# Nine small tiles requested earlier: where the large SBUF slots begin

## The chip, the core and the metric

The kernel runs on one core of a Trainium2 chip. The metric is the device time of one execution in microseconds, the median of several runs.

## What is computed

One hybrid decoder block over 256 positions of width 2048, all in fp32: a normed input and one wide projection, an S5 state-space branch and an attention branch over picked keys, both merged by gates, an output projection, a gated per-layer embedding and a last norm.

```
h = rms_norm(x, g_mix);  proj = h @ w_in            # 2048 -> 8272 columns
u, z_ssm, c_q, k, v, z_attn, k_idx, w_idx, gate_ssm, gate_attn = split(proj)
y_ssm  = s5_branch(u, ...) * silu(z_ssm)            # scan, gelu, y @ w_glu
o_ssm  = y_ssm @ w_ssm_out
cq     = rms_norm(c_q, g_q); q = cq @ w_uq; q_idx = cq @ w_uq_idx
y_attn = dsa_branch(q, k, v, q_idx, k_idx, w_idx) * silu(z_attn)
o_attn = y_attn @ w_attn_out
x = x + (sigmoid(gate_ssm) * o_ssm + sigmoid(gate_attn) * o_attn) @ w_o
e = rms_norm(p @ w_ple, g_ple_post)
x = x + sigmoid(rms_norm(x, g_ple) @ w_ple_gate) * e
return rms_norm(x, g_final)
```

## The kernel before

Every large product is made of fp32r matmuls in three parts: weights and activations are each split into a high and a low half, and high by high, high by low and low by high are accumulated in PSUM. The weights come as units of 128 x 1024 (512 KB, 4096 bytes in each partition). A unit is loaded by SyncE's queue into one of five `raw` buffers (L93 to L98), ScalarE rounds it into one of four `hi` buffers (L260), VectorE takes the rest into one of four `lo` buffers (L272), and TensorE uses both. All matmuls are recorded by one helper, `mm` (L140), all transposes by another (L148).

The main loop (L1175 to L1189) goes through the units one by one: the unit's matmuls, the `hi` of three units ahead, the deferred evictions, the `lo` of two units ahead, one more load, and then a share of the side threads (`pump`): the tables and the scan of the S5 branch (`s5_tables`, `s5_gen`, L805 and L893), the attention (`attn_gen`, L974). So each engine's order is fixed when the program is made.

A matmul here has a moving operand, which streams its columns, and a stationary one, loaded just before (LDWEIGHTS). Activations lie in the pool `cp`, in large slots that several tiles use in turn: XH and XL (the input's halves, later those of the residual sum), S1, S2, S5 of 16, 16 and 8 KB, and S4, S3, S7, kb, S6 of 8, 16, 16, 4 and 8 KB. There are two kinds of units:

- 256 columns: a block of output channels, the activations moving, 128 columns of weights stationary. XH and XL move in `block_k16` (28 blocks of 48 matmuls, before 388 us). In `block_small` (L343) S6 moves for the queries (`cq`, 16 blocks of 12 matmuls), and S7 for the GLU (`yg`, 16 blocks of 24).
- 512 columns: `block_tm` (L313), 128 positions of activations stationary, 512 columns of weights moving. XH and XL are stationary for the gates and for the last product; S3 for the SSM output (`ys`, 192 matmuls), S7 for the attention output (`ya`, 192), S5 for the embedding (`ph`, 48), and S2 with S3 for the output projection (`mh` in S2 and `ml` in S3, 384).

The first four of the last eight units keep their `hi` in S2 and their `lo` in S3 (`unit_tile`, L242).

A pool of one buffer per tag hands out bytes in the order in which tags are first requested, rounded up to 32, and a later request of the same tag gets the same bytes. A request issues no instruction. `const` (L66) and `slot` (L63) are such requests. The nine small tiles of the change are those of the last norms: `re_v`, `re_c`, `r2_v`, `r2_c` (L634 to L638), `r3v0`, `r3v1` (L690), `sqe` (L1086), `sq2` (L623), `sq3` (L657). Before, they are requested behind S6, `rcq_v`, `rcq_c` and `rowcq`.

Of the kernel before, what the change touches and what calls it, by code (L numbers as in the profile page):

```python
# [18 lines left out]
P = 128  # L19
# [10 lines left out]
NC = 4  # L30
# [13 lines left out]
def block_kernel(ctx: ExitStack, tc: tile.TileContext, A: dict, out: bass.AP):  # L44
# [14 lines left out]
    def nm(s):  # L59
        uid[0] += 1  # L60
        return f"{s}_{uid[0]}"

    def slot(tag, shape, dt=F32):  # L63
        return cp.tile(shape, dt, tag=tag, name=nm(tag))

    def const(s, shape, dt=F32):  # L66
        return cp.tile(shape, dt, tag=s, name=s)
# [142 lines left out]
    def spawn_first(gen):  # L210
        t = spawn(gen)
        threads.insert(0, threads.pop())
        return t
# [567 lines left out]
    def s5_powers():  # L781
        abr, abi = R["abar"][:, 0], R["abar"][:, 1]

        def cmul(i, xr, xi, yr, yi):
            t0, t1 = st_("er"), st_("eq")
            tt = TT
            tt(t0, xi, yi, ALU.mult)
            tt(t1, xr, yr, ALU.mult)
            tt(pre[:, i], t1, t0, ALU.subtract)
            tt(t0, xr, yi, ALU.mult)  # L790
            tt(t1, xi, yr, ALU.mult)
            tt(psi[:, i, 1], t1, t0, ALU.add)
            V.tensor_scalar(psi[:, i, 0], psi[:, i, 1], -1.0, None, ALU.mult)

        cmul(0, abr, abi, abr, abi)
        yield 1.2
        for i, a, b in ((1, 0, 0), (2, 1, 0), (3, 1, 1), (4, 3, 3), (5, 4, 3), (6, 4, 4)):
            cmul(i, pre[:, a], psi[:, a, 1], pre[:, b], psi[:, b, 1])
            yield 1.2

    def bc(ap, n):
        return ap.unsqueeze(-1).to_broadcast(list(ap.shape) + [n])


    def s5_tables():  # L805
        yield from s5_small()
        ab, f = R["abar"], R["f"]
        bp = slot("S4", [P, 2, 32, 32])
        nc.sync.dma_start(bp, A["sb"])
        ct = slot("S3", [P, 2, 2, 32, 32])  # L810
        nc.sync.dma_start(ct[:, 0, 0], A["sc"][:, 0])
        ci = slot("S7", [P, 2, 32, 32])
        nc.sync.dma_start(ci[:, 0], A["sc"][:, 1])
        yield 0.0
        bb = slot("S1", [P, 2, 32, 2, 32])

        def cmul_v(o, xr, xi, yr, yi, op):
            TT(o, xr, bc(yr, 32), ALU.mult)
            yield 1.14
            TT(ci[:, 1], xi, bc(yi, 32), ALU.mult)  # L820
            yield 1.14
            TT(o, o, ci[:, 1], op)
            yield 1.14

        br, bi = bp[:, 0], bp[:, 1]
        Br, Bi = bb[:, 0, :, 1, :], bb[:, 1, :, 1, :]
        abr, abi, nabi = ab[:, 0], ab[:, 1], ab[:, 2]
        yield from cmul_v(Br, br, bi, f[:, 0], f[:, 1], ALU.subtract)
        yield from cmul_v(Bi, bi, br, f[:, 0], f[:, 1], ALU.add)
        yield from cmul_v(bb[:, 0, :, 0, :], Br, Bi, abr, abi, ALU.subtract)  # L830
        yield from cmul_v(bb[:, 1, :, 0, :], Bi, Br, abr, abi, ALU.add)
        S.activation(ct[:, 1, 0], ci[:, 0], AF.Copy, scale=-1.0)
        R["ct"] = ct
        R["s5b"] = spawn_first(s5_states(bb))
        yield from cmul_v(ct[:, 0, 1], ct[:, 0, 0], ci[:, 0], abr, abi, ALU.subtract)
        yield from cmul_v(ct[:, 1, 1], ct[:, 0, 0], ct[:, 1, 0], nabi, abr, ALU.add)
        yield from s5_powers()
# [318 lines left out]

    R["xnorm"] = spawn(xnorm_gen(), 2)
    R["s5t"] = spawn(s5_tables(), 7)
    first_loads()
    S.activation(first, mhalf, AF.Copy)  # L1160
# [147 lines left out]
```

## Time and profile before

| | before |
|---|---|
| median of three runs | 798.55 us (798.19 to 799.98) |
| the profiled execution | 799.28 us |
| its span, first to last instruction | 797.3 us |
| TensorE (PE) busy | 776.6 us, 97% |
| VectorE (DVE) busy | 576.2 us, 72% |
| ScalarE (ACT) busy | 397.6 us, 50% |
| mean granted TensorE clock | 0.994 |

The span is what the profile sees; the 2.0 us beside it lie before and after. Busy time of PE overlaps itself, since one matmul starts before the one ahead has ended. How fast a stream of matmuls runs is read from the distance between their starts. [...]

### The profile page before, as it was taken

The page shows a single profiled execution, that of the slowest core. Times are in us where ns is not written, and L with a number is a line of the kernel's source. Part 1 is how long each engine was busy: PE and PEld are TensorE (multiplying, and loading weights), DVE is VectorE, ACT ScalarE, POOL GpSimd, SP SyncE. Part 2 cuts the span into 40 slices and gives each one's busy share as a digit, 9 for nine tenths or more (in the row PEclk, how much of TensorE's full clock was granted, in tenths as well). Part 3 has the DMA queues.
Part 4 walks back from the last instruction along what each step waited for, and adds up shares of the span by engine and source line. Part 5 has one row for each costly group of instructions (what it writes and reads, how often), then busy time and mean ns, then how long its engine had stood idle before and what let it go on. Part 6 is the DMA issues. An engine that isn't in the chain of part 4 may idle for free.

```text
span 797.3 us, 12926 instructions
## 1 busy us (share of the span) xinstructions
PE 776.6 (97%) x5080; PEld 674.5 (85%) x5080; DVE 576.2 (72%) x899; ACT 397.6 (50%) x544; POOL 8.8 (1%) x18
## 2 busy tenths in 40 slices
PE   8999999999997999999999999999999999999995
PEld 6999987777997888899999988887887888888885
DVE  6999964999999954455668887666678555456753
ACT  7544546543444744453455474544345454455642
POOL 0000000000000000000000000000000000000000
PEclk9999999999999999999999999999999999999998
DMA  8768775346662686634754556775866665556622
GB/s 318 284 211 228 232 222 179 116 162 208 213 209 92 204 259 212 220 112 146 244 179 153 189 167 221 232 247 193 266 218 219 228 204 185 176 181 195 217 86 106
DMA packets 52637, 158.08 MB, mean 198 GB/s; under 512 B 5984, under 2 KB 12128, under 8 KB 52192
## 3 DMA queue, kind: packets, MB, share of 16 engines
q1 hardware_dynamic: 47392, 150.15, 57.8%
q10 hardware_dynamic: 5184, 7.10, 2.5%
q8 instruction: 40, 0.66, 0.3%
q14 instruction: 21, 0.17, 0.1%
HBM read 147.79 MB, written 8.39 MB: 196 GB/s over the span
## 4 chain that ended last, share of the span: by engine, by line
PE 47%; issue 1%; DVE 1%; ACT 1%; DMA 1%; POOLq 0%; POOL 0%; DVEq 0%; ACTq 0%
PE main L140 44%; PE aux L140 2%; PE aux L148 1%; DMA zld<-za_d 1%; ACT S L697 0%; DVE lo L272 0%; DVE S L1087 0%; ACT hi L260 0%; ACT S L591 0%; DVE t L1045 0%; ACT S L650 0%; DVE S L649 0%; DVE S L648 0%; ACT S L645 0%; DVE S L651 0%
## 5 line engine op out<-in xcount | busy, mean ns | idle before, releaser
L272 DVE TENSOR_TENSOR lo<-raw,hi 128x1024 fp32r<-128x1024 f32 (+2 forms) x255 | 304.8, 1197 | 156.3 <-ACT hi L260 156.1
L260 ACT CAST hi<-raw 128x1024 fp32r<-128x1024 f32 (+2 forms) x255 | 261.4, 1031 | 302.9 <-PE main L140 268.3
L140 PE MATMUL main<-hi,S 128*128 128x512 f32 x544 | 175.6, 398 | 0.9 <-ACT S L1088 0.9
L140 PE MATMUL main<-lo,XH 128*128 128x512 f32 (+2 forms) x408 | 155.9, 382 | 2.4 <-DVE lo L272 2.4
L140 PE MATMUL main<-hi,XH 128*128 128x512 f32 (+2 forms) x408 | 156.9, 385 | 0.0
L140 PE MATMUL main<-hi,XL 128*128 128x512 f32 (+2 forms) x408 | 156.0, 382 | 0.0
L140 PE MATMUL main<-XH,hi 128*128 128x256 f32 x448 | 126.3, 282 | 2.7 <-ACT hi L260 2.7
L140 PE MATMUL main<-XH,lo 128*128 128x256 f32 x448 | 125.5, 280 | 1.9 <-DVE lo L272 1.9
L140 PE MATMUL main<-XL,hi 128*128 128x256 f32 x448 | 125.3, 280 | 0.0
L140 PEld LDWEIGHTS main<-hi,S 128*128 128x128 f32 x544 | 102.4, 188 | 24.8 <-ACT S L1088 1.6
L140 PE MATMUL main<-lo,S 128*128 128x512 f32 x272 | 107.5, 395 | 0.0
L140 PEld LDWEIGHTS main<-lo,XH 128*128 128x128 f32 x408 | 76.7, 188 | 19.0 <-DVE lo L272 4.6
L140 PEld LDWEIGHTS main<-hi,XH 128*128 128x128 f32 x408 | 76.6, 188 | 15.6
L140 PEld LDWEIGHTS main<-hi,XL 128*128 128x128 f32 x408 | 76.6, 188 | 14.3
L140 PEld LDWEIGHTS main<-XH,hi 128*128 128x128 f32 x448 | 84.9, 189 | 3.1 <-ACT hi L260 2.9
L140 PEld LDWEIGHTS main<-XH,lo 128*128 128x128 f32 x448 | 85.6, 191 | 2.1 <-DVE lo L272 2.1
L140 PEld LDWEIGHTS main<-XL,hi 128*128 128x128 f32 x448 | 85.0, 190 | 0.1
L140 PE MATMUL main<-S,hi 128*128 128x256 f32 x384 | 69.9, 285 | 0.1
L140 PEld LDWEIGHTS main<-lo,S 128*128 128x128 f32 x272 | 51.2, 188 | 11.1
L140 PEld LDWEIGHTS main<-S,hi 128*128 128x128 f32 x384 | 59.2, 189 | 1.7 <-issue 0.7
L140 PE MATMUL main<-S,lo 128*128 128x256 f32 x192 | 54.1, 282 | 0.0
L140 PEld LDWEIGHTS main<-S,lo 128*128 128x128 f32 x192 | 36.2, 189 | 0.0
(215 smaller groups left out, 656.4 us busy)
## 6 DMA issues: line engine op xcount, KB each, us to landing
raw<-in_wts_dram SPq DMA_DIRECT2D x247, 512.0 KB, 4.2
raw<-in_wvk_dram SPq DMA_DIRECT2D x8, 336.0 KB, 2.9
gs_d<-big ACTq DMA_DIRECT2D x8, 256.0 KB, 3.3
ga_d<-big ACTq DMA_DIRECT2D x8, 256.0 KB, 5.0
big<-gs_d SPq DMA_DIRECT2D x8, 256.0 KB, 4.4
big<-ga_d SPq DMA_DIRECT2D x8, 256.0 KB, 3.7
S<-in_grow_dram SPq DMA_DIRECT2D x2, 1024.0 KB, 7.5
big<-in_xtok_dram SPq DMA_DIRECT2D x8, 256.0 KB, 3.5
```

The source lines that it names most:

```text
L140: PE.matmul(o, l, r, start=start, stop=stop, **kw)
L148: PE.matmul(o, i, idn, is_transpose=True)
L260: S.copy(hi[:, o], src[:, o])
L272: TT(lo[:, o], src[:, o], his[u][:, o].bitcast(F32), ALU.subtract)
```

## The change

```diff
@@ def s5_tables() @@
         yield from s5_small()
         ab, f = R["abar"], R["f"]
+        for t in ("re_v", "re_c", "r2_v", "r2_c", "r3v0", "r3v1"):
+            const(t, [P, 2])
+        for t in ("sqe", "sq2"):
+            const(t, [P, 2, NC])
+        const("sq3", [P, 2, NC + 1])
         bp = slot("S4", [P, 2, 32, 32])
         nc.sync.dma_start(bp, A["sb"])
         ct = slot("S3", [P, 2, 2, 32, 32])
```

The nine tiles are requested once more, ahead of the first request of S4. They take 320 bytes there, and S4, S3, S7, kb, S6 and the three small tiles behind them move up by 320 bytes. What comes after the nine tiles' old place stays where it was. The first bytes within a partition, as the two programs have them:

```
slot                before   mod 512     after   mod 512
XH / XL      35104 / 51488       288      same       288
S1                   17728       320      same       320
S2 / S5      67872 / 84256       288      same       288
psi                  94496       288      same       288
S4                   98784       480     99104       288
S3                  106976       480    107296       288
S7                  123360       480    123680       288
kb                  139744       480    140064       288
S6                  143840       480    144160       288
rowcq               152096        32    152416       352
raw, hi, lo    from 153440       352      same       352
```

All tiles of `raw`, `hi` and `lo` are 4096 bytes apart. In both programs every engine has the same instructions in the same order, with the same waits.

## Rows read from the trace of the kernel before

**Rows 1.** The page: busy time of two engines, and the chain by line.
```profile
PE 776.6 (97%) x5080; PEld 674.5 (85%) x5080; DVE 576.2 (72%) x899; ACT 397.6 (50%) x544; POOL 8.8 (1%) x18
...
PE 47%; issue 1%; DVE 1%; ACT 1%; DMA 1%; POOLq 0%; POOL 0%; DVEq 0%; ACTq 0%
```

**Rows 2.** PE's waits from 388 to 700 us: us in total, times, longest.
```profile
PE main L140 <- ACT S L1088: 0.9, 1, 0.9
PE aux L148 <- DVE t L1045: 0.2, 1, 0.2
```

**Rows 3.** Line 140 in six windows: count, durations, first and last start, forms.
```profile
L140 PE MATMUL main<-XH,hi x139: 276/276/276, 35.8 to 82.7; 128*128 128x256 f32 x139
...
L140 PE MATMUL main<-XH,lo x74: 281/281/281, 207.9 to 233.7; 128*128 128x256 f32 x74
...
L140 PE MATMUL main<-XH,lo x57: 281/281/281, 346.9 to 366.7; 128*128 128x256 f32 x57
...
L140 PE MATMUL main<-S,lo x34: 282/285/287, 389.9 to 401.7; 128*128 128x256 f32 x34
...
L140 PE MATMUL main<-S,lo x52: 279/281/285, 430.8 to 449.0; 128*128 128x256 f32 x52
...
L140 PE MATMUL main<-lo,S x42: 392/400/400, 607.1 to 636.0; 128*128 128x512 f32 x42
```

**Rows 4.** Pieces of the chain that ended last: start, length, what, instructions.
```profile
506.76 14.00 PE main L140 x60
...
542.51 4.54 DMA zld<-za_d
...
566.94 11.19 PE main L140 x48
...
579.00 11.14 PE main L140 x48
...
638.88 22.18 PE main L140 x96
...
661.93 22.47 PE main L140 x96
...
685.27 22.11 PE main L140 x96
...
708.26 68.70 PE main L140 x300
```

**Rows 5.** Timeline of PE around 593.5 us: start, length, what.
```profile
591.78 0.40 PE L140 MATMUL main<-lo,S 128*128 128x512 f32 x1
...
593.18 0.40 PE L140 MATMUL main<-lo,S 128*128 128x512 f32 x1
...
593.88 0.39 PE L140 MATMUL main<-lo,S 128*128 128x512 f32 x1
...
595.94 0.39 PE L140 MATMUL main<-lo,S 128*128 128x512 f32 x1
```

**Rows 6.** Windows: us; busy of PE, PEld, DVE, ACT, POOL; clock, DMA, GB/s.
```profile
253.00:258.00 5.00, 0.50 (x2) 0.30 (x2) 4.96 (x8) 4.78 (x7) 0.00 (x0) 1.00 0.00 0
258.00:262.00 4.00, 3.97 (x20) 3.97 (x21) 4.00 (x6) 3.39 (x6) 0.00 (x0) 0.57 0.51 164
...
438.00:448.00 10.00, 10.00 (x86) 10.00 (x86) 9.90 (x26) 4.79 (x7) 0.66 (x1) 1.00 0.61 206
...
468.00:478.00 10.00, 10.00 (x48) 7.54 (x46) 9.79 (x21) 6.40 (x9) 0.00 (x0) 1.00 0.65 205
```

**Rows 7.** DVE: the scan's first half, its second half, slots in 206 to 262.
```profile
L915 DVE TENSOR_TENSOR S<-S,pre 128x1024 f32<-128x1024 f32 x3 | 3.7, 1223 | 0.1
...
L915 DVE TENSOR_TENSOR S<-S,pre 128x1024 f32<-128x1024 f32 x3 | 3.7, 1217 | 0.0
...
206.00:262.00 56.00, 37.42 (x72) 0.97 0.54 172
```

## The prediction

> **What bounds the kernel now.** I read the page first, then TensorE's waits, then the chain of work that ended last, and only then single stretches. On the page PE is busy 97% of the span, VectorE 72%, and the chain is a list of PE pieces with hardly anything between them [rows 1]. The waits say the same of the part of the program that uses the moved slots: from 388 to 700 us PE's matmuls waited 1.1 us in total for other engines [rows 2]. So from 388 us on the pace of back-to-back matmuls is the pace of the kernel, and a nanosecond saved per matmul is saved for good, unless another engine is found right behind.
>
> The pace is the distance from one matmul's start to the next, not its duration (276 to 400 ns, overlapped). In a row of line 140 for a window it is last start minus first start, divided by the count less one, and by three, since one operand pair in three has that name. In a piece of the chain it is length by count. Two forms matter, and each runs both on slots that move and on slots that stay:
>
> - 256 columns, the slot as the moving operand, the weight pieces hi and lo as the stationary one. On XH and XL (byte 288 modulo 512) 138 x 3 intervals from 35.8 to 82.7 us give 113.3 ns, the same form on the same bytes from 207.9 to 233.7 us gives 117.8, and from 346.9 to 366.7 us 117.9 [rows 3]. On S6 and S7 (byte 480) it is 119.2 (389.9 to 401.7 us, 33 x 3) and 119.0 (430.8 to 449.0 us, 51 x 3) [rows 3].
> - 512 columns, the slot as the stationary operand, hi and lo moving. On XH and XL 300 matmuls in 68.70 us: 229.0 ns. On S3 60 in 14.00 us: 233.3. On S7 48 in 11.19 and 48 in 11.14 us: 233.1 and 232.1. In the output projection, whose high halves lie in S2 (byte 288) and low halves in S3 (480), 96 in 22.18 and 96 in 22.47 us: 231.0 and 234.1 [rows 4].
>
> What makes these differ? Width, type, line and clock are alike. The row that tells most is a place where only the stationary slot changes in the middle of a stream: by the program's order the stationary operand is S7 (480) up to 593.5 us and S5 (288) from there, and the weights stay where they are. The starts run 591.78 to 593.18, six intervals of 233 ns, and then 593.88 to 595.94, nine of 229 [rows 5]. S5 is another slot than XH, 48 KB further on, and still has XH's pace. The pool also rotates hi and lo through four buffers 4096 bytes apart with no trace of it in the pace. So I take the byte modulo 512 as what counts.
>
> **The change, part by part.** The nine requests issue no instruction, and the order and the waits on all five engines are those of before. Nothing is added to pay for; what changes is the start byte of S4, S3, S7, kb and S6 (480 to 288 modulo 512), and of rcq_v, rcq_c and rowcq. Weights, XH, XL, S1, S2, S5 and the evictions' buffers stay.
>
> *256 columns.* The query units run on S6, 16 blocks of 12, 192 matmuls; the GLU units on S7, 16 of 24, 384. After the change their operands start on the bytes of XH and the weights. XH has two paces there, and I can't say beforehand which one a stretch will fall into: a stretch keeps the pace it enters with, and entries follow each interruption by small matmuls. Bounds: all at 117.8 gives 192 x 1.4 + 384 x 1.2 = 0.7 us, all at 113.3 gives 192 x 5.9 + 384 x 5.7 = 3.3 us. Before 388 us, of the 1344 matmuls of this form, about 560 run at the slow pace (66 us of starts: 22 to 34, 206 to 235 and 347 to 372 us, of which [rows 3] shows the cores of the latter two) and 780 at the fast one, a mean of 115.2. I take that mean: 192 x 4.0 + 384 x 3.8 = 2.2 us.
>
> *512 columns.* All XH stretches have 229.0, with no second pace. The SSM output (S3) has 192 matmuls, 192 x 4.3 = 0.8 us. The attention output (S7) 192 x 3.6 = 0.7 us. The output projection has 384: its first stretch runs at 235 (607.1 to 636.0 us, 41 x 3, read to a tenth of a us; I take 234) [rows 3], then 231.0 and 234.1 [rows 4], and the last piece, 96 in 22.11 us [rows 4] with some 38 of XH at its end, leaves 231. Weighted 232.8, so 384 x 3.8 = 1.5 us. Together 3.0 us. The 48 matmuls on S5 have the pace already.
>
> *The last eight units.* Half of their weights are kept in S2 and S3 as moving operands; S3 goes from 480 to 288, the byte of XH itself. That pair of equal bytes exists there already (S2 with XH). At most 48 matmuls of 256 columns by the 5 ns that the paces of this width differ: 0.2 us either way, taken as nothing.
>
> *Other engines.* VectorE reads two operands from slots in the scan. In the first half of it E and W both start at 480, in the second E is S1 (320) and W 480: 1223 and 1217 ns for the same 1024 elements [rows 7]. So its pace hardly knows the bytes; taken as nothing, with 0.5% of the scan's 37.4 us of slot work between 206 and 262 us [rows 7], 0.2 us, either way. [...]
>
> *What is late next.* Where PE gets faster, lo must keep up. VectorE is busy 9.90 of 10 us from 438 to 448 and 9.79 of 10 from 468 to 478 [rows 6]. The code keeps two units of lead, so a full 10 us that would have to shrink by 0.4 us is carried by the lead; if it isn't, the 256-column gain from there on is lost, at most the GLU's 1.4 us. Further down the chain holds one transfer, 4.54 us for a zld tile [rows 4]; it hangs on work that PE itself releases and so moves with it, at no cost or gain.
>
> Sum: 2.2 + 3.0 = 5.2 us. The profiled execution took 799.28 us (span 797.3 and 2.0 around it); it would become 794.1. It lies 0.7 us above the median of the three runs, 798.55, and from that the forecast is 793.3 us, 0.65% less. A measurement of this kernel can tell about 0.2% (1.6 us) from no change.
>
> **The rivals.** *Bytes don't matter to TensorE.* Its two streams would then be free of each other and the paces above would come from something else, say from what the other engines do in those stretches. Time: 798.5. For it: the same XH bytes show 113.3 and 117.8, so something beside bytes is at work. Against it: [rows 5], where the pace switches with the slot and nothing else, and a 229.0 that holds across 68.70 us of differing company [rows 4]. [...] Chance 9%; another 1% for a cancelling drift of the fast stretches before 388 us (780 matmuls at +4.5 ns would give back 3.5 us).
>
> *Only the 512-column half pays.* The query and GLU stages fall into the slow pace of XH, or VectorE's full stretches eat what they save: 3.0 us and a bit, 795.3. For it: 9.90 of 10 us in [rows 6], and the direct entry from another width at 206 us went into the slow pace. Against it: the lead of two units, and the entry at 34 us, after small matmuls as there are between the GLU units, which went into the fast one [rows 3]. Chance 20%.
>
> *Slower: VectorE pays for equal bytes.* E in S7, W in S4 and the power tables in psi would all start at 288, and in the second half W at 288 against S1 at 320. In the full stretch from 206 to 262 us any loss goes straight into PE's wait at 253 [rows 6]. Of its 37.4 us of slot work, 18% (6.8 us) is the point from which the kernel gets slower by over 0.2%; at 25%, 9.4 us less the 5.2, it would take 802.7. Against it: E and W had equal bytes before, at 0.5% [rows 7]. Chance 4%, with what else may turn up.
>
> **How the numbers follow.** Main case 66%, the half case 20%: faster 0.86. Same 0.10, slower 0.04. Range: the low end takes the fast pace throughout, 6.3 us, and about one us of slow stretches before 388 us that may turn fast, 791.0; the high end is the half case with two us of the fast stretches turned slow, 797.2.
>
> **What would show it.** In the profile after, the pieces on S3, S7 and of the output projection should read 229 ns by length over count, as XH's; if they stay at 232 to 234, bytes modulo 512 were not the cause. The query and GLU stages should read 113.3 or 117.8 and nothing between but mixtures. VectorE's two scan halves should keep 1217 to 1223 ns, and PE's gap at 253 us its size. The forecast is wrong if PE's waits for lo grow between 430 and 490 us, or if stretches before 388 us change their pace by more than the moved ones gain.

## The result and the profile after

| | before | after |
|---|---|---|
| median of five runs | 799.18 us (798.19 to 800.71) | 793.74 us (793.06 to 794.93) |
| the profiled execution | 799.28 us | 793.06 us |
| its span | 797.3 us | 791.0 us |
| mean granted TensorE clock, a share of the full one | 0.994 | 0.993 |

The ratio of after to before is 0.9936, with a 95% interval of 0.9925 to 0.9947: 5.4 us less, where 5.2 had been worked out. The forecast was 793.3 us, 0.65% less; it came to 0.64% less.

The page of after, to be held against [rows 1]: busy time by engine, and the chain by engine.

```profile
PE 770.6 (97%) x5080; PEld 671.8 (85%) x5080; DVE 576.0 (73%) x899; ACT 397.6 (50%) x544; POOL 8.8 (1%) x18
...
PE 48%; issue 1%; ACT 1%; DVE 1%; POOLq 0%; POOL 0%; ACTq 0%
```

The chain as it is printed begins at 388 us, so 48% of the span is nearly all of it. The counts are the same on every engine, and so is, to 0.2 us, the time of VectorE and ScalarE. Only PE became shorter, by 6.0 us, and its weight loads by 2.7. PE's waits from 388 to 700 us are down to one row, the first of [rows 2]:

```profile
PE main L140 <- ACT S L1093: 0.9, 1, 0.9
```

So what the matmuls saved was not handed to a wait. The chain of after, in pieces (start, length, what, instructions), answers to [rows 4]; the first piece holds the last 72 matmuls of the queries and the first 48 of the GLU, the second 168 of the GLU:

```profile
400.77 13.62 PE main L140 x120
...
427.63 19.26 PE main L140 x168
...
503.04 13.76 PE main L140 x60
...
562.26 11.00 PE main L140 x48
574.13 11.00 PE main L140 x48
...
633.23 21.99 PE main L140 x96
...
656.09 21.99 PE main L140 x96
...
678.95 21.98 PE main L140 x96
...
701.80 68.67 PE main L140 x300
```

The same two pieces before:

```profile
402.61 14.24 PE main L140 x120
...
430.22 20.13 PE main L140 x168
```

Length by count: S6 and S7 as moving operand 13.62 / 120 = 113.5 ns a matmul (before 118.7), S7 alone 19.26 / 168 = 114.6 (before 119.8; both with a first interval of 0.22 us behind small matmuls, and from 430.40 us on every interval of after is 113 or 114 ns), S3 13.76 / 60 = 229.3 (before 233.3), S7 as stationary operand 11.00 / 48 = 229.2 (before 233.1 and 232.1), the output projection 21.99 / 96 = 229.1 (before 231.0 and 234.1). XH at the end keeps 228.9. All 512-column stretches now have one pace.

The timeline of PE at the place of [rows 5], where the stationary operand changes from S7 to S5 near 588.5 us (start, length, what):

```profile
586.77 0.39 PE L140 MATMUL main<-lo,S 128*128 128x512 f32 x1
...
588.14 0.39 PE L140 MATMUL main<-lo,S 128*128 128x512 f32 x1
...
590.89 0.39 PE L140 MATMUL main<-lo,S 128*128 128x512 f32 x1
```

Six intervals from the first to the second row, on S7, give 228.3 ns, twelve more to the third, nearly all on S5, 229.2. Before, the pace switched here from 233 to 229. Now nothing is left to switch.

Where the 6.3 us of the two spans lie follows from the starts of the same chain pieces in both profiles:

| stretch | before, us | after, us | saved |
|---|---|---|---|
| up to the queries | 389.17 | 388.02 | 1.15 |
| queries and GLU | 77.40 | 75.02 | 2.38 |
| last gates, SSM and attention outputs, most of S5's units | 131.36 | 129.84 | 1.52 |
| from there to the output projection's second stretch | 7.44 + 33.51 | 7.43 + 32.92 | 0.60 |
| the rest of the output projection | 68.51 | 67.70 | 0.81 |
| last product and end | 89.91 | 90.07 | -0.16 |

The first row is not the change's. 0.5 us of it is a gap of PE at 91 us, 1.41 us from one matmul on XH to the next for 0.91 after, 0.3 of it a wait for ScalarE; `all_moved` below has that wait of 0.3 us too, with all the distances of after. The rest lies in XH's 256-column stretches, whose bytes did not move; the experiment `after_again` below shows that they differ between executions of one program. Without it the spans differ by 5.15 us.

### The profile page after: what moved, and what is told of

Read it like the earlier page. It is cut to its first block, busy times and chain, and to the rows that moved or that the text cites. A ratio compares the mean times of both kernels' runs of the same rounds, so it can differ in the third digit from the quotient of the medians.

```text
span 791.0 us, 12926 instructions
## 1 busy us (share of the span) xinstructions
PE 770.6 (97%) x5080; PEld 671.8 (85%) x5080; DVE 576.0 (73%) x899; ACT 397.6 (50%) x544; POOL 8.8 (1%) x18
## 4 chain that ended last, share of the span: by engine, by line
PE 48%; issue 1%; ACT 1%; DVE 1%; POOLq 0%; POOL 0%; ACTq 0%
PE main L140 44%; PE aux L140 2%; PE aux L148 1%; ACT S L697 0%; DVE lo L272 0%; DVE S L1092 0%; ACT hi L260 0%; ACT S L591 0%; ACT S L650 0%; DVE S L648 0%; DVE S L649 0%; ACT S L645 0%; DVE S L651 0%; POOLq L1308 0%; ACT S L1093 0%
## 5 line engine op out<-in xcount | busy, mean ns | idle before, releaser
L140 PE MATMUL main<-S,hi 128*128 128x256 f32 x384 | 67.5, 280 | 0.1
```

The costliest lines, as they stand in the source:

```text
L140: PE.matmul(o, l, r, start=start, stop=stop, **kw)
```

## Experiments

The expectations number the theories. Theory 1: the pace of a matmul on TensorE follows the distance in bytes between the start of the activations' slot and the start of the weights' buffer. Theory 2: it follows the slot's own start byte. Theory 3: bytes don't matter to TensorE. Below, *d* is the weights' start minus the slot's start, modulo 512. In the kernel before d is 64 for XH, XL, S2, S5 and 384 for S3, S6, S7; after, it is 64 for all.

**Weights moved instead of slots.** From before; a last request in the slots' pool puts 192 bytes ahead of the weights' pool, which lies behind it, so raw, hi and lo start at 32 modulo 512 (the evictions' buffers, further on, move along). Slots stay where they were: d becomes 64 for S3, S6, S7 and 256 for XH, XL, S2, S5.

```diff
     finish_half(1)
+    const("padw", [P, 48])
```

> The kernel before with all weight buffers 192 bytes further on, at byte 32 modulo 512; every slot stays (XH, XL, S2, S5 at 288, S3, S6, S7 at 480). So the weights stand 64 above S3, S6 and S7, and 256 above XH, XL, S2, S5. Theory 1 (the distance from slot to weights sets the pace): the queries and the GLU run at 113.3 or 117.8 ns, S3's and S7's 512-column matmuls at 229, as in the changed kernel, although their slots have not moved; XH's stretches get a new pace, which I can't say. Theory 2 (the slot's own byte sets it): all as before, 119 and 233 on S3, S6, S7, 113 to 118 and 229 on XH; 799 us. Theory 3 (bytes don't matter to TensorE): as before, 799 us.

Measured: 797.91 us, ratio to before 0.9987 (0.9977 to 0.9996). Pieces of its chain, in the order queries, GLU, S3, S7, output projection (twice), XH:

```profile
406.18 13.62 PE main L140 x120
...
433.04 19.25 PE main L140 x168
...
508.26 13.75 PE main L140 x60
...
568.01 11.00 PE main L140 x48
...
639.20 22.20 PE main L140 x96
...
662.27 22.20 PE main L140 x96
...
708.30 68.17 PE main L140 x300
```

The slots on byte 480 have the paces of after, to 0.01 us a piece, though not one of them moved. XH, which didn't move either, changed both its paces: 68.17 / 300 = 227.2 ns at 512 columns, less than ever before, and at 256 columns this row (line 140 in 36 to 83 us: count, durations, first and last start)

```profile
L140 PE MATMUL main<-XH,hi x131: 283/283/366, 35.9 to 82.7; 128*128 128x256 f32 x131
```

gives 46.8 us by 130 x 3 = 120.0 ns, where XH had 113.3. What S3, S6, S7 and the wide matmuls on XH gained, XH's 1344 narrow ones gave back, which is why the total hardly moved. So the slot's byte alone is not the cause, nor anything that stays fixed when only the weights move. One thing came out unexplained: in the output projection, which alternates between S2 (d = 256) and S3 (d = 64), 22.20 / 96 = 231.3 ns is slower than either distance has alone (227.2 and 229).

**Both moved.** From after; 192 bytes ahead of XH, so every slot that these matmuls read starts at 480 and the weights at 32. All distances are those of after, none of these start bytes is.

```diff
+    const("padx", [P, 48])
     xgh = slot("XH", [P, KT, T], F32R)
     xgl = slot("XL", [P, KT, T], F32R)
```

> The changed kernel with XH, XL and all behind them, weights included, 192 bytes further on: slots at 480, weights at 32 modulo 512, still 64 above. Theory 1 (distance): the paces and the time of the changed kernel, 793.7 us within 1.6. Theory 2 (the slot's own byte, 480 being the bad one): all stretches of 256 columns at 119 ns and of 512 at 233, 1920 x 4.6 ns and 1872 x 3.7 ns over the changed kernel, some 809 us. Theory 3: 794 to 799 us.

Measured: 794.63 us, ratio 0.9947 (0.9928 to 0.9965), overlapping after's interval. The pieces of the chain are after's to 0.02 us (13.62 for the queries, 13.76 for S3, 11.00 for S7, 21.99 in the output projection, 68.69 for XH). All slots at the byte that looked slow before run at the good pace. Theory 2 has fallen; theory 1 stands both ways.

**The nine tiles behind S3.** From before; the requests stand behind the one for S3, so S7, kb and S6 move and S4 and S3 don't. A part of the change alone.

```diff
         ct = slot("S3", [P, 2, 2, 32, 32])
+        for t in ("re_v", "re_c", "r2_v", "r2_c", "r3v0", "r3v1"):
+            const(t, [P, 2])
+        for t in ("sqe", "sq2"):
+            const(t, [P, 2, NC])
+        const("sq3", [P, 2, NC + 1])
```

> The nine tiles requested behind S3 instead of ahead of S4: S7, kb and S6 move to 288 as in the change, S4 and S3 stay at 480. Theories 1 and 2: the queries and the GLU gain 2.4 us and the attention output 0.7 as in the changed kernel; the SSM output (S3) stays at 233 ns and the output projection (S2 with S3) at 231 to 234, so 2.2 us of the change's gain are missing: 795 to 796.5 us. Theory 3: no such split by slot; the time lies where the company of other engines puts it.

Measured: 796.29 us, ratio 0.9969 (0.9954 to 0.9984). Chain pieces: queries, GLU, S3, S7, output projection (three times):

```profile
400.80 13.62 PE main L140 x120
427.66 19.26 PE main L140 x168
...
503.27 14.00 PE main L140 x60
...
563.63 11.00 PE main L140 x48
...
635.23 22.18 PE main L140 x96
...
658.28 22.47 PE main L140 x96
...
681.62 22.11 PE main L140 x96
```

S6 and S7 have after's lengths; S3 and the output projection have before's, to the hundredth (14.00, 22.18, 22.47, 22.11 in [rows 4]). The gain is the sum of separate gains, one for each slot and form. The median is 2.6 us below before's; the sum has 2.2 + 0.7 for S6 and S7.

**Scans of the distance.** From after; hi and lo get four fixed buffer pairs with pads between them, so that successive units of 24 (or 12) matmuls on XH run at four distances in turn, in one program. The evictions' `t` gets eight buffers for nine, to make room.

```diff
-        return wp.tile([P, 1024], F32R, tag=tag, name=nm(tag))
+        return wp.tile([P, 1024], F32R, tag=f"{tag}{u % 4}", name=nm(tag), bufs=1)
...
+    for i, n in enumerate((0, 16, 16, 16)):
+        if n:
+            wp.tile([P, n], F32, tag=f"pad{i}", name=f"pad{i}", bufs=1)
+        for t in ("hi", "lo"):
+            wp.tile([P, 1024], F32R, tag=f"{t}{i}", name=f"{t}pre{i}", bufs=1)
```

The first pad is 0, 64, 8 and 72 elements of 4 bytes in the four kernels: distances 64, 128, 192, 256; 320, 384, 448, 0; 96, 160, 224, 288; 352, 416, 480, 32.

> The changed kernel with its four pairs of weight buffers at four distances above the slots: 64, 128, 192 and 256 bytes modulo 512, by unit number modulo 4 (raw buffers behind them; eight instead of nine buffers for the evictions' products). Theory 1: within each stretch on XH the pace goes through four values in turn, and the units at 64 have 113 to 118 ns (256 columns) and 229 (512). Theories 2 and 3: one pace for all four. The time itself is not the question; somewhere from 785 to 810 us.

> As scan_64_256, with the four pairs of weight buffers 320, 384, 448 and 0 bytes above the slots (modulo 512). Theory 1 (the distance from slot to weights sets the pace): 384 gives what S3, S6 and S7 had before, 119 ns (256 columns) and 232.5 (512); 0 gives what the last eight units have where two equal bytes meet, 120 and 227; 320 and 448 are unknown, and if the pace depended on the distance without its sign they would be those of 192 (118, 233) and 64 (113 to 118, 229). Theory 2 (the slot's own byte): one pace, 113 to 118 and 229.

> As scan_64_256, with distances 96, 160, 224 and 288 (odd multiples of 32, so that a slot and the weights differ in their place within 64 bytes). If only the distance in steps of 64 counts, each behaves as a neighbour: 113 to 120 ns and 227 to 233. If the place within 64 bytes counts, a pace outside of those ranges shows.

> As scan_96_288, with distances 352, 416, 480 and 32. The same two possibilities: within 113 to 120 ns and 227 to 233, or outside.

Measured, one execution of each: 801.65, 801.83, 806.29 and 806.26 us, beside 798.6 to 798.9 for before. The paces stand in the timelines. The last matmul of five successive 256-column units, in the kernel with 64 to 256 (start, length, what):

```profile
45.93 0.28 PE L140 MATMUL main<-XH,lo 128*128 128x256 f32 x1
...
48.66 0.28 PE L140 MATMUL main<-XH,lo 128*128 128x256 f32 x1
...
51.50 0.28 PE L140 MATMUL main<-XH,lo 128*128 128x256 f32 x1
...
54.33 0.28 PE L140 MATMUL main<-XH,lo 128*128 128x256 f32 x1
...
57.21 0.28 PE L140 MATMUL main<-XH,lo 128*128 128x256 f32 x1
```

From each row to the next is the length of a unit: 2.73, 2.84, 2.83 and 2.88 us, for d = 64, 128, 192 and 256. The same five rows where d is 320, 384, 448 and 0:

```profile
45.87 0.28 PE L140 MATMUL main<-XH,lo 128*128 128x256 f32 x1
...
48.60 0.28 PE L140 MATMUL main<-XH,lo 128*128 128x256 f32 x1
...
51.44 0.28 PE L140 MATMUL main<-XH,lo 128*128 128x256 f32 x1
...
54.27 0.28 PE L140 MATMUL main<-XH,lo 128*128 128x256 f32 x1
...
57.15 0.28 PE L140 MATMUL main<-XH,lo 128*128 128x256 f32 x1
```

2.73, 2.84, 2.83 and 2.88 again, though each unit is 256 bytes further off. All sixteen distances, as the length of a unit by its matmuls, in ns:

| d modulo 256 | 0 | 32 | 64 | 96 | 128 | 160 | 192 | 224 |
|---|---|---|---|---|---|---|---|---|
| 256 columns (24) | 120.2 | 118.5 | 113.7 | 118.8 | 118.2 | 119.6 | 117.9 | 116.7 |
| 512 columns (12) | 228.3 | 233.3 | 230.3 | 234.2 | 232.9 | 233.3 | 232.9 | 233.6 |

These units lie in 36 to 83 us (256 columns) and 293 to 320 us (512). In every column two distances 256 bytes apart were run, and there their units agree to 0.01 us. So the period is 256 bytes, not 512. The sign counts: 64 and 192 differ. The best distance is another one for each form: 64 for 256 columns, 0 for 512. (A unit's length includes its passage to a neighbour with another distance; streams that stay at 0 or at 64 have 227.2 and 229.0 at 512 columns.)

**After once more.** The changed kernel itself, beside a new set of runs of before.

> The changed kernel once more, beside the two below: 793.7 us, 0.9936 of before.

Measured: 794.23 us, ratio 0.9945 (0.9932 to 0.9957). The stretch of XH from 347 us, in the profile of after and then in this one (line 140: count, durations, first and last start):

```profile
L140 PE MATMUL main<-XH,hi x57: 276/276/276, 346.7 to 365.8; 128*128 128x256 f32 x57
```

```profile
L140 PE MATMUL main<-XH,lo x55: 281/281/281, 346.8 to 365.9; 128*128 128x256 f32 x55
```

One program, the same bytes: 19.1 / (56 x 3) = 113.7 ns in one execution, 19.1 / (54 x 3) = 117.9 in the other. At 206 us before and after differ in the same way, on bytes that the change leaves alone: [rows 3] have 281 ns and 117.8 there, after has 276 and 113.0 up to 222 us. Such choices make up the other 0.6 us ahead of the queries. By the starts of the same matmuls in both profiles, after gained 0.6 us between 206 and 235 us and 0.8 between 347 and 372, and lost 0.5 between 235 and 268 us and 0.3 between 332 and 347, for the most part in stretches where it had 117.8 ns and before 113.3.

**Wide weights at distance 0.** From after; a hi or lo buffer is 256 bytes longer, and a unit of 512 columns uses it from element 48 (192 bytes) on, so that wide units have d = 0 modulo 256 and narrow ones keep 64. `t` has seven buffers.

```diff
-        return wp.tile([P, 1024], F32R, tag=tag, name=nm(tag))
+        o = 0 if units[u][3] in narrow else 48
+        return wp.tile([P, 1088], F32R, tag=tag, name=nm(tag))[:, o:o + 1024]
```

> The changed kernel, with weight buffers 256 bytes longer, in which units of 512 columns start 192 bytes later: there the weights stand 256 above the slots, in units of 256 columns 64 as before (seven instead of nine buffers for the evictions' products). By the scans (the distance counts, modulo 256; 0 is best for 512 columns at 227.2 ns, 64 for 256 columns): 1872 matmuls x 1.8 ns less than the changed kernel, 790.4 us, unless the two buffers less add a wait. If the scans' mixtures misled, 229 stays and 793.7 us.

Measured: 790.65 us (790.33 to 791.15), ratio to before 0.9899 (0.9884 to 0.9914), 3.6 us below the 794.23 of the changed kernel on the same chip. Chain pieces: S3, S7, output projection, XH:

```profile
502.09 13.62 PE main L140 x60
...
561.93 10.93 PE main L140 x48
...
632.52 21.81 PE main L140 x96
...
700.58 68.06 PE main L140 x300
```

226.9 to 227.7 ns in all of them, the queries and GLU as in after (13.61 and 19.26 us). This beats both kernels.

**Slots at distance 0.** From before; the nine tiles move ahead to other places, and instead of the weights the slots are placed: S2, S3, S5, and by an offset of 64 bytes the late tiles in S7, XH and XL, start where the weights do modulo 256. Only wide units (and the last eight) use them so; a few other requests change places to give these bytes. The weights come to lie 256 bytes further on, which is the same place modulo 256.

```diff
+    def behind(tag, off):
+        return slot(tag, [P, KT * T + 16], F32R)[:, off:off + KT * T]
...
-        ya = slot("S7", [P, 2, 8, T], F32R)
+        ya = behind("S7", 16).rearrange("p (a h t) -> p a h t", a=2, t=T)
```

> The weights where they are, and the tiles that only serve 512 columns moved to their distance 0 modulo 256 (S2, S3, S5, and inside their slots the attention output, and the residual's halves in XH and XL); those of 256 columns stay 64 below. Only the gates' 720 matmuls of 512 columns keep 229 ns: some 1150 x 1.8 ns less than the changed kernel, 791.7 us; the last eight units' 256-column matmuls stay at 120 ns.

Measured: 791.22 us (790.89 to 793.19), ratio 0.9912 (0.9899 to 0.9926). Chain pieces: S7, output projection, XH:

```profile
562.00 10.90 PE main L140 x48
...
632.44 21.78 PE main L140 x96
...
700.40 68.03 PE main L140 x300
```

The same paces by moving the other operand. The gates at the middle of the kernel stay at 64, and the two times, 791.22 and 790.65 us, have overlapping intervals of their ratios.

## Why the prediction was right, and where not

**What bounds the kernel.** The reading held: from 388 to 700 us TensorE's pace is the kernel's. A saving of some 4 ns a matmul on 192 + 192 + 384 matmuls of 512 columns and 576 of 256 came through whole, since no other engine was close enough behind. PE's waits there got no longer, and VectorE's full stretch had room. The windows of after that answer to [rows 6] (us; busy time of PE, PEld, DVE, ACT, POOL; clock, DMA share, GB/s):

```profile
434.00:444.00 10.00, 10.00 (x90) 10.00 (x89) 9.86 (x28) 4.38 (x7) 0.00 (x0) 1.00 0.56 184
...
464.00:474.00 10.00, 10.00 (x48) 7.60 (x47) 9.79 (x21) 6.93 (x9) 0.00 (x0) 1.00 0.55 175
```

Ten microseconds of the same stage now hold 90 matmuls for 86, with VectorE at 9.86 for 9.90, and PE did not wait for it. That the lead of two units carried this, as the prediction had it, fits and was not measured by itself.

**512 columns.** 3.0 us were worked out. The stretch of S3 and S7 gave 1.52 us (0.8 + 0.7 in the sum), the output projection 0.60 + 0.81 = 1.41 (1.5 in the sum): 2.9. Of the 1.52 us 0.2 are a wait and not pace (see late next, below).

**256 columns.** 2.2 us were taken, from the mean of XH's two paces, with 0.7 and 3.3 as bounds. Measured over the whole stretch: 2.38. S6 fell into the fast pace, S7 for some 240 of its 384 matmuls; the GLU units at 415, 423 and from 448 us on have 117.8 ns. That the mean came so close is luck, since nothing in the sum said which pace a stretch enters. It was not chance from one execution to the next: from the first query to the end of the GLU all seven profiles with S6 and S7 at d = 64 modulo 256 throughout have 75.0 us by their chains (after, after_again, weights_moved, all_moved, behind_s3, wide_at_0, slots_at_0), and before has 77.4. The 119.2 ns that the prediction read for S6, from starts in tenths of a us, were two paces: 84 matmuls of 120.0 ns from 390.59 to 400.67 us, and 69 of 118.7 from 402.69 to 410.88, behind two small matmuls.

**The last eight units.** The one term with a wrong size and sign. It stood at nothing, within 0.2 us; the end of the kernel became 0.16 us longer. The prediction argued that the pair of equal bytes "exists there already". The scan shows what equal bytes mean at 256 columns: d = 0 is the slowest place, 120.2 ns, while S3 against XH before had 480 - 288 = 192, at 117.9. The 48 matmuls that were counted took 0.08 us longer. Another 0.10 us is in the last 24, which no argument of the prediction covers: they use hi and lo buffers, whose bytes did not move. Their first and last start, before and then after:

```profile
785.26 0.28 PE L140 MATMUL main<-hi,XH 128*128 128x256 f32 x1
...
787.87 0.28 PE L140 MATMUL main<-hi,XL 128*128 128x256 f32 x1
```

```profile
778.87 0.28 PE L140 MATMUL main<-hi,XH 128*128 128x256 f32 x1
...
781.58 0.28 PE L140 MATMUL main<-hi,XL 128*128 128x256 f32 x1
```

23 intervals of 113.5 ns became 23 of 117.8: the two paces of d = 64 once more, entered from other neighbours. Here the weights move and XH is stationary, the other way round than in the scan. So the two paces at d = 64 go with 256 columns, whichever operand moves; and so does the slow place at 0, where the 48 matmuls on S2 and S3 have 119 to 120 ns in after (23 intervals each from 770.30 to 773.06 and from 776.01 to 778.75 us), for 118 before, with S3 at 192.

**Why bytes matter.** Here the prediction was right in its paces and wrong in its rule. It took the slot's byte modulo 512 as the cause, from S7 against S5 in [rows 5]. Those rows can't tell a slot's byte from its distance to the weights, because no weight moved in that program. The runs with the weights moved, and with both, show the distance; the scans show modulo 256. For this change both rules give the same numbers. They would not for the next one: by the prediction's rule there is nothing left to gain once all slots agree, and the distance gave another 3.6 us.

**The rivals.** *Bytes don't matter to TensorE* is out: with nothing but one pad ahead of the weights, nearly all long stretches of the kernel change their pace (XH at 256 columns from 113.3 to 120.0 ns, S3 at 512 from 233.3 to 229.2), and one and the same pair of instructions has 227.2 to 234.2 ns at 512 columns at different distances. *Only the 512-column half pays* is out by the 2.38 us that the queries and the GLU gave. *VectorE pays for equal bytes* is out by the rows of the S5 branch's scan in after; its first half, to be held against the 1223 ns of [rows 7] (line, engine, operation, tiles, count; busy us, mean ns; idle before):

```profile
L920 DVE TENSOR_TENSOR S<-S,pre 128x1024 f32<-128x1024 f32 x3 | 3.7, 1222 | 0.1
```

The second half has 1218 ns for 1217. VectorE's slots moved by the same 320 bytes (in the second half W against S1, which stayed), and its time hardly by one part in a thousand. PE's two gaps around 253 us, from one matmul's start to the next, were 3.01 and 2.21 us and are 3.13 and 2.21.

**What was said of late next.** The `zld` transfer of 4.54 us in [rows 4] has left the chain. The prediction counted that as neither cost nor gain. It was worth 0.2 us here: the second row of [rows 2], PE's wait for `t` (L1045) behind that transfer, is gone. `all_moved`, with the same distances, still has that wait of 0.2 us, so the distances alone did not remove it.

**What stays open.** Why the distance acts, and why with a period of 256 bytes: the runs show the paces, not a mechanism. What decides which of two paces a stretch of 256 columns enters. Why a stream that alternates between two distances can be slower than either (231.3 ns for 227.2 and 229 in the output projection with the weights moved). None of these was tried further.

## What to carry to other kernels

Where matmuls run back to back, read the pace from starts, slot by slot and width by width: the same form on two slots is an experiment that the kernel has already made. Then place operands by the distance between activations and weights, modulo 256 bytes here, and for each width by itself (64 for 256 columns, 0 for 512, in these fp32r streams; but in the slow pace of 64, 117.8 ns, 224 is better with 116.7), by padding a pool or by offsets into a buffer. A rule read from one program covers only what that program varies; move the other operand once before building on it.

## What was not expected of the hardware

- The pace of a stream of matmuls depends on where its two operands start relative to each other: at 512 columns 227.2 ns (d = 0), 229.0 (64) and 232 to 234 elsewhere, at 256 columns 113.3 to 120.2, with a period of 256 bytes and no symmetry (64 is not 192).
- The best distance for one width is the worst for the other: d = 0 is fastest at 512 columns (227.2 ns) and slowest at 256 (120.0).
- At d = 64 the 256-column stream has two stable paces, 113.3 and 117.8 ns, on the same addresses; the same program chose differently at 347 us in two executions. At d = 128 (S6 before) there were two as well, 120.0 and 118.7.
- VectorE's work on the same slots showed none of it: 1217 to 1223 ns for 128x1024, before and after.
